# A one-core decoder layer on Trainium2: wide and narrow products of each split weight in strict alternation, high weights 192 bytes further in their tiles, and four smaller edits

## The chip, the core and the metric

One Trainium2 chip; the kernel runs on one of its cores. That core has TensorE (PE in the profile; its weight loads are the rows marked PEld), VectorE (DVE), ScalarE (ACT), GpSimd (POOL) and SyncE (SP), which issues most of the DMAs. Each engine works through its own queue in order and waits for the others by semaphores. The metric is the device time of one execution in microseconds, as a median over runs.

## The reference, cut to what matters

One layer over 256 positions of width 2048, everything in float32:

```python
h = rms_norm(x, pre_mix_norm)
gq, gk, gv, gz, ga, gb, mq, mk, mv = split(h @ w_in)          # 2048 x 7184
mix = concat([gdn(gq, gk, gv, gz, ga, gb), moba(mq, mk, mv)]) @ w_out   # 8 + 8 heads of 128
x = x + rms_norm(mix, post_mix_norm)
ca = cross_attention(rms_norm(x, pre_mem_norm), rms_norm(mem, mem_kv_norm))  # 4 heads, 256 tokens
x = x + rms_norm(ca, post_mem_norm)
f = square(relu(rms_norm(x, pre_mlp_norm) @ w_up)) @ w_down     # hidden 8192
x = x + rms_norm(f, post_mlp_norm)
```

Nearly all arithmetic is in the products with `w_in`, `w_out`, `w_up` and `w_down`.

## The kernel before

**Split products.** A float32 operand goes to TensorE as two fp32r parts, a high one (the rounded value) and a low one (the rest), and each product is high times high, high times low and low times high. Activations lie with their high and low part side by side, 256 + 256 columns. Weights arrive in float32 and are split on the way: `Stream` (line 51) cuts all weights into 434 units of 512 KB (the first four of 256 KB), loads each to `wraw` by SP, casts it to `whi` on ACT (L69) and subtracts it to `wlo` on DVE (L71). There are 5 `wraw`, 4 `whi` and 4 `wlo` buffers; a unit is asked for three units ahead (`AHEAD`).

**Two kinds of products.** Where the output is wanted transposed (`a_tile` and `a_group`, lines 118 to 140: the input projection but for `mv`, `w_mk`, `w_mq`, `w_up`), the weight is the stationary operand: `whi` streams 512 columns (both parts of the activation), `wlo` 256 columns (the high part alone). I call these two a wide and a narrow product, and together a pair: a pair is one 128x128 block of a weight. `products` (line 102) issues all wide ones of a unit first, then all narrow ones: eight and eight for a unit of 1024 columns. In `b_group` (`w_out`, `w_mv`, `w_mo`, `w_down`, `mv`) the activation is stationary and the weight streams, three products of 512 columns (256 in the halves of a last group) per block; the change leaves their order as it is.

**Order.** TensorE's queue stands as the code is written (`manual_schedule` of PE). DVE, ACT, SP and POOL are ordered by the framework's scheduler, but for what `pin` keeps in program order. Side work runs in generators on the list `bg`, which `tick` moves one step after each unit: the delta rule, the block attention `moba`, the memory's norm `mem_in`, and `natural`, which adds a residual in natural layout.

**Begin of the MLP.** After `w_mo`, `residual` (line 754) makes the row factors by Newton steps on DVE, scales the four 512-column slices of the result by them on ACT (L768, L772; DVE L769 for half of one), transposes two blocks at a time on TensorE (L778: one "pair of transposes" is four instructions), adds them to `x1` on DVE (L782) and splits the normed value (`norm_split`: ACT L231 high, DVE L232 low). The first `next(res)` makes the factors and scales slice 3; three more `next(res)` put four pairs of transposes in the queue with the idle products (`ones`) ahead of them; then `a_group` multiplies the first `w_up` unit (blocks 12 and 13), with one more pair of transposes behind each unit.

**Norm rows.** `row_load` (line 262) loads a norm weight to all partitions and scales it by the constant RS8 on ACT (L266).

## Time and profile before

| | us |
|---|---|
| median of 3 runs | 1317.57 (1316.19 to 1318.88) |
| the profiled execution | 1317.31 |
| its span, first to last instruction | 1315.5 |
| PE busy | 1295.0 of the span |
| DVE busy | 873.0 |
| ACT busy | 664.7 |
| time of the DMA queue with the weights | 56.3% of 16 engines |
| granted TensorE clock, mean | 0.995 |

The profiled execution took 0.26 us less than the median, and 1.8 us of it lie outside the span. A row of a list of groups gives line, engine, operation, names as out<-in, shapes and count, then busy time and the mean (or least, median, greatest) duration in ns. A row of a timeline gives start and length of a merged run in us, and in brackets the engine's idle time before it and what ended it. Ends of matmuls are modelled; spacings are therefore read from starts.

### The profile page before, as it was taken

What the parts mean: (1) busy time and instruction counts of PE and PEld (TensorE: products, weight loads), DVE (VectorE), ACT (ScalarE), POOL (GpSimd) and SP (SyncE); (2) the same over time, 40 slices, a digit from 0 to 9 for tenths busy, and PEclk for the clock granted to TensorE, in tenths of its full rate; (3) what the DMA queues carried; (4) which work ended last, traced back from release to release, by engine and by line L of the source; (5) the groups of instructions that cost most, each with busy time, mean ns of one, the idle gap of its engine ahead of it and who ended that gap; (6) DMA issues with size and microseconds to landing.
All of it is one profiled execution on the core that took longest, in us unless ns stands there. A gap on an engine that the chain in (4) does not pass through costs nothing.

```text
span 1315.5 us, 18643 instructions
## 1 busy us (share of the span) xinstructions
PE 1295.0 (98%) x6945; PEld 1115.1 (85%) x6945; DVE 873.0 (66%) x1528; ACT 664.7 (51%) x1028; POOL 35.4 (3%) x64
## 2 busy tenths in 40 slices
PE   9999999999999999999999999999999999999997
PEld 8888888898887788888888888888888888888886
DVE  8988879867575759759966654444466666554555
ACT  7655544525555757657644444444444444443442
POOL 1010010100000000000000000000000000000000
PEclk9999999999999999999999999999999999999998
DMA  8655565624446865744665656666655565666662
GB/s 308 190 183 182 187 192 172 194 82 144 144 130 224 290 213 169 246 154 145 196 190 191 191 178 195 196 192 195 196 193 189 184 190 191 214 198 193 193 190 86
DMA packets 72378, 246.25 MB, mean 187 GB/s; under 512 B 10408, under 2 KB 11872, under 8 KB 71904
## 3 DMA queue, kind: packets, MB, share of 16 engines
q1 hardware_dynamic: 70016, 239.27, 56.3%
q0 software_dynamic: 2272, 5.80, 1.5%
q8 instruction: 54, 0.88, 0.3%
q14 instruction: 36, 0.29, 0.1%
HBM read 241.35 MB, written 3.69 MB: 186 GB/s over the span
## 4 chain that ended last, share of the span: by engine, by line
PE 66%; DMA 3%; DVE 2%; ACT 1%; issue 1%; DVEq 0%; SPq 0%; ACTq 0%; POOLq 0%
PE mm L49 63%; PE ax L49 2%; DMA xs<-in_memT_dram 2%; DMA t<-rd 1%; DMA wraw<-in_wout_dram 1%; DVE wlo L71 1%; PE ax L778 0%; DVE ca L981 0%; ACT whi L69 0%; DMA rd<-t 0%; ACT m L231 0%; PE ax L886 0%; DVE fd L965 0%; DVE yg L681 0%; ACT ca L772 0%
## 5 line engine op out<-in xcount | busy, mean ns | idle before, releaser
L71 DVE TENSOR_TENSOR wlo<-wraw,whi 128x1024 fp32r<-128x1024 f32 (+1 forms) x434 | 528.1, 1219 | 371.7 <-ACT whi L69 369.6
L69 ACT ACTIVATE whi<-wraw 128x1024 fp32r<-128x1024 f32 (+1 forms) x434 | 456.2, 1054 | 519.2 <-PE mm L49 341.4
L49 PE MATMUL mm<-h,whi 128*128 128x512 f32 x1024 | 256.8, 393 | 0.0
L49 PE MATMUL mm<-whi,fp 128*128 128x512 f32 (+1 forms) x816 | 240.3, 377 | 0.0
L49 PEld LDWEIGHTS mm<-h,whi 128*128 128x128 f32 x1024 | 184.2, 189 | 33.2 <-DVE h L232 0.2
L49 PE MATMUL mm<-x,whi 128*128 128x512 f32 x768 | 201.0, 404 | 1.1 <-ACT whi L69 1.1
L49 PEld LDWEIGHTS mm<-whi,fp 128*128 128x128 f32 x816 | 150.2, 188 | 28.1
L49 PEld LDWEIGHTS mm<-x,whi 128*128 128x128 f32 x768 | 140.7, 191 | 27.6 <-ACT whi L69 1.5
L49 PE MATMUL mm<-wlo,fp 128*128 128x512 f32 (+1 forms) x408 | 153.7, 377 | 0.0
L49 PEld LDWEIGHTS mm<-h,wlo 128*128 128x128 f32 x1024 | 139.7, 190 | 10.0
L49 PE MATMUL mm<-h,wlo 128*128 128x256 f32 x1024 | 142.8, 282 | 0.0
L49 PEld LDWEIGHTS mm<-x,wlo 128*128 128x128 f32 x768 | 105.2, 190 | 8.0
L49 PE MATMUL mm<-x,wlo 128*128 128x256 f32 x768 | 107.4, 282 | 0.0
L49 PEld LDWEIGHTS mm<-wlo,fp 128*128 128x128 f32 x408 | 76.8, 188 | 14.2
L49 PE MATMUL mm<-whi,f 128*128 128x512 f32 (+1 forms) x272 | 81.0, 377 | 0.0
L49 PEld LDWEIGHTS mm<-whi,f 128*128 128x128 f32 x272 | 50.1, 188 | 9.4
L49 PE MATMUL mm<-wlo,f 128*128 128x512 f32 (+1 forms) x136 | 51.3, 377 | 0.0
L113 ACT ACTIVATE right<-mm 128x256 f32<-128x256 f32 x120 | 44.9, 378 | 4.6 <-PE mm L49 2.5
L49 PE MATMUL mm<-whi,ym 128*128 128x512 f32 x128 | 42.5, 393 | 0.9 <-ACT whi L69 0.9
L49 PE MATMUL mm<-whi,yg 128*128 128x512 f32 x128 | 41.9, 391 | 0.4 <-ACT whi L69 0.4
L381 DVE SCALAR_TENSOR_TENSOR t<-xc,cl,t 128x256 f32<-128x256 f32 x72 | 34.6, 481 | 2.6 <-ACT t L379 1.5
L49 PE MATMUL mm<-whi,x 128*128 128x512 f32 x96 | 31.8, 396 | 0.0
(359 smaller groups left out, 1246.8 us busy)
## 6 DMA issues: line engine op xcount, KB each, us to landing
wraw<-in_wup_dram SPq DMA_DIRECT2D x128, 512.0 KB, 3.9
wraw<-in_wdn_dram SPq DMA_DIRECT2D x128, 512.0 KB, 4.4
wraw<-in_win_dram SPq DMA_DIRECT2D x110, 512.0 KB, 4.0
wraw<-in_wout_dram SPq DMA_DIRECT2D x32, 512.0 KB, 5.0
wraw<-in_wmk_dram SPq DMA_DIRECT2D x8, 512.0 KB, 4.5
wraw<-in_wmq_dram SPq DMA_DIRECT2D x8, 512.0 KB, 4.2
wraw<-in_wmv_dram SPq DMA_DIRECT2D x8, 512.0 KB, 5.1
wraw<-in_wmo_dram SPq DMA_DIRECT2D x8, 512.0 KB, 3.7
```

Of the source, the lines that this page charges most:

```text
L49: TE.matmul(o, l, r, start=start, stop=stop, skip_group_check=skip)
L69: cast = S.activation(hi, r, AF.Copy)
L71: sub = V.tensor_tensor(lo, r, hi.bitcast(F32), OP.subtract)
L113: S.activation(t, o[:, T:], AF.Copy)
L381: V.scalar_tensor_tensor(y, c[:, i:i + T], cw[:, 4 * ch + i:4 * ch + i + 1], y, OP.mult, OP.add)
```

## The change

Five edits. (1) `three` takes the place of `products`: wide and narrow products alternate, one by one. (2) A `whi` tile has 1088 columns instead of 1024, and where the high weight is stationary it lies 48 columns (192 bytes) further in. (3) The MLP's first unit goes in three passes of 256 columns (high weight on the activation's high part, low weight on it, high weight on the low part), behind one pair of transposes and onto banks that a product with a tile of zeros has begun; ACT's scaling of a slice is put behind the first pair of transposes of the slice before; four units' casts and subtractions are pinned instead of one. (4) The norm rows stay unscaled and RS8 goes into the product that uses them. (5) `mem_in` splits its memory tokens in steps of two, `moba` waits one step more at its start, and a constant is put into `ssr` by a memset instead of an addition.

```diff
-            for n, (src, a, fine) in enumerate(plan):
+            for src, a, fine, off in plan:
                 step = 1 if fine else a // 2
-                s.units += [(n, src, a, k, step, fine) for k in range(0, a, step)]
+                s.units += [(src, a, k, step, off) for k in range(0, a, step)]
...
             nc.sync.dma_start(r, v[:, k:k + step])
-            hi = wp.tile([P, step, c], F32R, tag="whi", name="whi", bufs=NHI)
+            hi = wp.tile([P, 1024 + 64], F32R, tag="whi", name="whi", bufs=NHI)
+            hi = hi[:, off:off + step * c].rearrange("p (a c) -> p a c", a=step)
             cast = S.activation(hi, r, AF.Copy)
             lo = wp.tile([P, step, c], F32R, tag="wlo", name="wlo", bufs=NLO)
             sub = V.tensor_tensor(lo, r, hi.bitcast(F32), OP.subtract)
...
-    def products(steps):
-        for o, w, act, k, first, last in steps:
-            mm(o, w[0], act[2][k], start=first, stop=False)
-        for o, w, act, k, first, last in steps:
-            mm(o[:, :T], w[1], act[0][k], start=False, stop=last)
+    def three(o, whi, wlo, act, k, first, last):
+        mm(o, whi, act[2][k], start=first, stop=False)
+        mm(o[:, :T], wlo, act[0][k], start=False, stop=last)
...
         while k < KT:
-            u = ws.next()
-            products([(o, w, act, k + i, k + i == 0, k + i == KT - 1) for i, w in enumerate(u)])
-            k += len(u)
+            for w in ws.next():
+                three(o, *w, act, k, k == 0, k == KT - 1)
+                k += 1
             tick()
         return o
-    def a_group(act, order, pre=None):
...
-        o = [mmps() for _ in range(4)]
+    def a_group(act, order, pre=None, begun=None):
+        o = begun or [mmps() for _ in range(4)]
         n = 0
         while n < KT:
             u = ws.next()
             if pre:
                 pre(n)
-            cut = lambda w, c: [x[:, c * P:(c + 1) * P] for x in w]
-            products([(o[c], cut(w, c), act, order[n + i], n + i == 0, n + i == KT - 1)
-                      for i, w in enumerate(u) for c in range(4)])
-            n += len(u)
+            if begun and n == 0:
+                for kind in range(3):
+                    for i, w in enumerate(u):
+                        for c in range(4):
+                            cs = slice(c * P, (c + 1) * P)
+                            mm(o[c][:, T:] if kind == 2 else o[c][:, :T], w[kind % 2][:, cs],
+                               act[kind // 2][order[i]], start=False, stop=False)
+                    if kind == 1:
+                        pre(n)
+                n += len(u)
+                tick()
+                continue
+            for w in u:
+                for c in range(4):
+                    cs = slice(c * P, (c + 1) * P)
+                    three(o[c], w[0][:, cs], w[1][:, cs], act, order[n], n == 0, n == KT - 1)
+                n += 1
...
+    zero = cp.tile([P, P], F32R, name="zero")
     V.memset(ones, 1.0)
+    V.memset(zero.bitcast(F32), 0.0)
...
-    plan = [(win[i], 4, i == 0) for i in range(4)]
+    plan = [(win[i], 4, i == 0, 48) for i in range(4)]
     for what, h in TURNS:
         i, n = {"mv": (24 + 4 * h, 4), "kq": (2 * h, 2), "m": (32 + 2 * h, 2), "v": (16 + h, 1), "z": (48 + h, 1)}[what]
-        plan += [(win[i + j], 4 if what == "mv" else KT, False) for j in range(n)]
-    plan += [(wout[i], 4, False) for i in range(16)]
-    plan += [(wmk[i], KT, False) for i in range(HM)]
-    plan += [(wmq[i], 4, False) for i in range(HM)]
-    plan += [(wmv[i], 4, False) for i in range(4)]
-    plan += [(wmo[i], 4, False) for i in range(4)]
+        plan += [(win[i + j], *((4, False, 0) if what == "mv" else (KT, False, 48))) for j in range(n)]
+    plan += [(wout[i], 4, False, 0) for i in range(16)]
+    plan += [(wmk[i], KT, False, 48) for i in range(HM)]
+    plan += [(wmq[i], 4, False, 48) for i in range(HM)]
+    plan += [(wmv[i], 4, False, 0) for i in range(4)]
+    plan += [(wmo[i], 4, False, 0) for i in range(4)]
     for half in range(2):
-        plan += [(wup[32 * half + i], 4 if half == 0 and i < 4 else KT, False) for i in range(32)]
-        plan += [(wdn[32 * half + i], 4, False) for i in range(32)]
+        plan += [(wup[32 * half + i], 4 if half == 0 and i < 4 else KT, False, 48) for i in range(32)]
+        plan += [(wdn[32 * half + i], 4, False, 0) for i in range(32)]
...
         nc.sync.dma_start(w, bass.AP(tensor=rows.tensor, offset=rows.offset + i * D, ap=[[0, P], [1, D]]))
-        S.activation(w, w, AF.Copy, scale=RS8)
         return w
...
         ym = ap_.tile([P, 2, H, T], F32R, tag="ym", name="ym")
         def moba(h, q, k):
+            yield
             yield
...
-        ssr = small(10, "ssr")
+        ssr = small(12, "ssr")
         V.memset(ssr, 0.0)
+        V.memset(ssr[:, 5::6], D * EPS)
...
             V.tensor_reduce(ssq, ssr.rearrange("p (t c) -> p t c", t=2), AX.X, OP.add)
-            V.tensor_scalar(ssq, ssq, D * EPS, None, OP.add)
             r = newton8(ssq, name)
             for _ in range(lag):
                 yield
-            for n, c in enumerate((3, 0, 1, 2)):
...
-                        S.activation(m[t], m[t], AF.Copy, scale=r[:, t:t + 1])
+            m = {c: [src[:, t, 512 * c:512 * (c + 1)] for t in range(2)] for c in range(4)}
+            for i in range(2):
+                hc = slice(i * T, (i + 1) * T)
+                src0, src1 = [(o[i][0] if len(o) > 1 else o[0][0][:, hc]) for o in last]
+                S.activation(m[3][0][:, hc], src0, AF.Copy, scale=r[:, 0:1])
+                V.tensor_scalar(m[3][1][:, hc], src1, r[:, 1:2], None, OP.mult)
+            for c, then in ((3, 0), (0, 1), (1, 2), (2, None)):
                 for i in range(2):
                     yield
...
-        def natural(dst, other, i, r):
+                    if i == 0 and then is not None:
+                        for t in range(2):
+                            pin(S.activation(m[then][t], m[then][t], AF.Copy, scale=r[:, t:t + 1]))
...
-                    V.tensor_tensor(x, x, w[:, cs], OP.mult)
+                    late(V.scalar_tensor_tensor(x, x, RS8, w[:, cs], OP.mult, OP.mult))
                     V.tensor_tensor(x, x, o, OP.add)
...
                     sq = ld2.tile([P, 4, T], F32, tag="msq", name="msq", bufs=2) if q else acc
-                    prep(hm, memT, n_kv, ld2, 4 * q, 4, sq)
+                    xs = ld2.tile([P, 4, T], F32, tag="xs", name="xs", bufs=2)
+                    nc.sync.dma_start(xs, memT[q])
+                    for k in range(4):
+                        norm_split(hm, xs[:, k], n_kv, 4 * q + k)
+                        if k % 2:
+                            yield
+                    S.activation(sq, xs, AF.Square)
                     yield
                     if q:
                         V.tensor_tensor(acc, acc, sq, OP.add)
-                    yield
...
-                ssm.append(sm.tile([P, T], F32, tag="mmb", name="mmb"))
+                ssm.append(p2.tile([P, T], F32, tag="mmb", name="mmb"))
...
-        for _ in range(10):
+        for _ in range(9):
             mm(idle[:, 0:P], ones, ones)
-        for _ in range(3):
-            next(res)
+        begun = []
+        for n in range(4):
+            if n == 2:
+                next(res)
+            begun.append(mmps())
+            mm(begun[n], zero, chl[:, 0, 0:2].rearrange("p h t -> p (h t)"), stop=False)
...
-        ws.pin, ws.ahead = 1, AHEAD
-        o_first = a_group(h2, late, lambda n: next(res, None))
+        ws.pin, ws.ahead = 4, AHEAD
+        o_first = a_group(h2, late, lambda n: next(res, None), begun)
...
-        bg.append(natural(x2n, lambda t, cs: mix[:, t, cs], 1, r2))
+        bg.append(natural(x2n, lambda t, cs: mix[:, t, cs], 1, r2, pin))
...
-                    V.tensor_tensor(fw[t, c], fd[:, t, cs], wrow[:, cs], OP.mult)
+                    V.scalar_tensor_tensor(fw[t, c], fd[:, t, cs], RS8, wrow[:, cs], OP.mult, OP.mult)
```

TensorE in the up projection, at any unit (`h` is the normed activation). Before:

```order
L49 MATMUL mm<-h_6036,whi 128x512 x8
L49 MATMUL mm<-h_6036,wlo 128x256 x8
L49 MATMUL mm<-h_6036,whi 128x512 x8
L49 MATMUL mm<-h_6036,wlo 128x256 x8
L49 MATMUL mm<-h_6036,whi 128x512 x8
```

The same place now:

```order
L49 MATMUL mm<-h_6037,whi 128x512
L49 MATMUL mm<-h_6037,wlo 128x256
L49 MATMUL mm<-h_6037,whi 128x512
L49 MATMUL mm<-h_6037,wlo 128x256
L49 MATMUL mm<-h_6037,whi 128x512
L49 MATMUL mm<-h_6037,wlo 128x256
```

Nothing but the order within a unit moved: the count of wide and of narrow products is the same.

TensorE at the begin of the MLP (`ca` is the attention's result, transposed against `ident`). Before:

```order
L49 MATMUL ax<-ones 128x128 x10
L778 MATMUL ax<-ident,ca 128x128 x16
L49 MATMUL mm<-h_6036,whi 128x512 x8
L49 MATMUL mm<-h_6036,wlo 128x256 x8
L778 MATMUL ax<-ident,ca 128x128 x4
L49 MATMUL mm<-h_6036,whi 128x512 x8
```

And now:

```order
L49 MATMUL ax<-ones 128x128 x9
L49 MATMUL mm<-chl,zero 128x512 x2
L788 MATMUL ax<-ident,ca 128x128 x4
L49 MATMUL mm<-chl,zero 128x512 x2
L788 MATMUL ax<-ident,ca 128x128 x4
L49 MATMUL mm<-h_6037,whi 128x256 x8
L49 MATMUL mm<-h_6037,wlo 128x256 x8
L788 MATMUL ax<-ident,ca 128x128 x4
L49 MATMUL mm<-h_6037,whi 128x256 x8
L788 MATMUL ax<-ident,ca 128x128 x4
L49 MATMUL mm<-h_6037,whi 128x512
```

Two pairs of transposes stand ahead of the first weight product instead of four, and two more within the first unit.

ACT there, from the scaling of slice 3 on. Before:

```order
L768 ACTIVATE ca<-mm,x_6040 128x256 x2
L772 ACTIVATE ca<-ca,x_6040 128x512 x2
L231 ACTIVATE h_6036<-x_4445,cl 128x256 x3
L772 ACTIVATE ca<-ca,x_6040 128x512 x2
L231 ACTIVATE h_6036<-x_4445,cl 128x256 x3
L69 ACTIVATE whi<-wraw 128x1024 x2
```

And now:

```order
L780 ACTIVATE ca<-mm,x_6040 128x256 x2
L244 ACTIVATE h_6037<-x_4447,cl 128x256 x2
L797 ACTIVATE ca<-ca,x_6040 128x512 x2
L70 ACTIVATE whi<-wraw 128x1024 x2
L244 ACTIVATE h_6037<-x_4447,cl 128x256 x4
L797 ACTIVATE ca<-ca,x_6040 128x512 x2
```

The splits of blocks 12 and 13 moved ahead of the scaling of slice 0, and two casts ahead of the splits of blocks 14 and 15. DVE's queue there, before:

```order
L782 SCALAR_TENSOR_TENSOR x_4445<-ax,n_sc,x_4445 128x256 x3
L232 SCALAR_TENSOR_TENSOR h_6036<-x_4445,cl,h_6036 128x256 x2
L782 SCALAR_TENSOR_TENSOR x_4445<-ax,n_sc,x_4445 128x256
L232 SCALAR_TENSOR_TENSOR h_6036<-x_4445,cl,h_6036 128x256
L782 SCALAR_TENSOR_TENSOR x_4445<-ax,n_sc,x_4445 128x256 x2
```

And now:

```order
L792 SCALAR_TENSOR_TENSOR x_4447<-ax,n_sc,x_4447 128x256 x3
L245 SCALAR_TENSOR_TENSOR h_6037<-x_4447,cl,h_6037 128x256 x2
L792 SCALAR_TENSOR_TENSOR x_4447<-ax,n_sc,x_4447 128x256 x2
L72 TENSOR_TENSOR wlo<-wraw,whi 128x1024 x2
L245 SCALAR_TENSOR_TENSOR h_6037<-x_4447,cl,h_6037 128x256 x3
```

The two subtractions that belong to those casts now stand ahead of the low part of block 14. At the memory's norm, the queues of ACT and DVE stand as before but for their line numbers.

## Rows read from the trace of the kernel before

**Rows 1.** The page: busy us of each engine, share of the span, instructions.

```profile
PE 1295.0 (98%) x6945; PEld 1115.1 (85%) x6945; DVE 873.0 (66%) x1528; ACT 664.7 (51%) x1028; POOL 35.4 (3%) x64
```

**Rows 2.** Timeline of PE in the up projection: start us, us, what.

```profile
640.44 2.00 PE L49 MATMUL mm<-h,whi 128*128 128x512 f32 x8
642.28 1.11 PE L49 MATMUL mm<-h,wlo 128*128 128x256 f32 x8
...
648.82 2.00 PE L49 MATMUL mm<-h,whi 128*128 128x512 f32 x8
```

**Rows 3.** By tile: count, durations in ns (least/median/greatest), first and last start.

```profile
L49 PE MATMUL mm<-h,whi x1024: 387/393/496, 596.7 to 1129.0; 128*128 128x512 f32 x171
L49 PE MATMUL mm<-x,whi x768: 387/393/774, 5.0 to 393.6; 128*128 128x512 f32 x192
L49 PE MATMUL mm<-whi,f x272: 277/389/396, 777.3 to 1271.9; 128*128 128x512 f32 x120, 128*128 128x256 f32 x16
```

**Rows 4.** By tile, the same view for the low parts.

```profile
L49 PE MATMUL mm<-h,wlo x1024: 277/283/283, 598.6 to 1130.0; 128*128 128x256 f32 x171
```

**Rows 5.** Timeline of PE in the `mv` products, 512 columns throughout.

```profile
38.16 0.39 PE L49 MATMUL mm<-wlo,x 128*128 128x512 f32 x1
...
40.20 0.39 PE L49 MATMUL ax<-wlo,x 128*128 128x512 f32 x1
```

**Rows 6.** Timeline of PE in the last `w_down` group: six of 512 columns, twelve of 256.

```profile
1272.00 0.40 PE L49 MATMUL mm<-whi,fp 128*128 128x512 f32 x1
...
1273.16 0.50 PE L49 MATMUL mm<-whi,fp 128*128 128x512 f32 x2
...
1273.98 0.40 PE L49 MATMUL mm<-whi,fp 128*128 128x256 f32 x2
...
1274.70 0.52 PE L49 MATMUL mm<-whi,fp 128*128 128x256 f32 x2
```

**Rows 7.** Timeline of PE at the start of the program.

```profile
12.27 2.11 PE L49 MATMUL mm<-x,whi 128*128 128x512 f32 x8 [0.72 <-ACT whi L69]
...
15.17 2.01 PE L49 MATMUL mm<-x,whi 128*128 128x512 f32 x8
```

**Rows 8.** Timeline of DVE in the same stretch.

```profile
12.25 1.23 DVE L71 TENSOR_TENSOR wlo<-wraw,whi 128x1024 fp32r<-128x1024 f32 x1 [1.02 <-ACT whi L69]
...
15.59 1.22 DVE L71 TENSOR_TENSOR wlo<-wraw,whi 128x1024 fp32r<-128x1024 f32 x1
```

**Rows 9.** Timeline of all engines at the begin of the MLP.

```profile
594.37 1.33 ACT L772 ACTIVATE ca<-ca,x 128x512 f32<-128x512 f32 x2
...
594.89 1.27 DVE L782 SCALAR_TENSOR_TENSOR x<-ax,n_sc,x 128x256 f32<-128x256 f32 x3 [0.25 <-PE ax L778]
595.60 1.30 ACT L231 ACTIVATE h<-x,cl 128x256 fp32r<-128x256 f32 x3
...
596.67 2.11 PE L49 MATMUL mm<-h,whi 128*128 128x512 f32 x8
...
599.22 2.00 ACT L69 ACTIVATE whi<-wraw 128x1024 fp32r<-128x1024 f32 x2
...
599.93 1.40 PE L49 MATMUL mm<-h,whi 128*128 128x512 f32 x5
```

**Rows 10.** Chain of waits in order of time, at 446 us.

```profile
445.78 9.56 DMA wraw<-in_wout_dram
```

**Rows 11.** Timeline of ACT there, and of PE behind it.

```profile
454.10 1.92 ACT L266 ACTIVATE wrow<-wrow 128x2048 f32<-128x2048 f32 x1 [7.10 <-DMA wrow<-in_rows_dram]
...
457.01 0.49 PE L49 MATMUL mm<-whi,yg 128*128 128x512 f32 x1 [0.44 <-ACT whi L69]
```

**Rows 12.** Timeline of PE at a fall of the clock.

```profile
273.10 1.10 PE L49 MATMUL ax<-tr,ga 128*128 128x64 f32 x8 [0.84 <-DVE t L550]
274.01 3.63 PE L49 MATMUL mm<-x,whi 128*128 128x512 f32 x8
```

**Rows 13.** A window there: length, busy us (count) of PE, PEld, DVE, ACT, POOL, then the granted clock.

```profile
274.10:277.40 3.30, 3.30 (x9) 2.57 (x9) 0.86 (x4) 0.00 (x0) 0.00 (x0) 0.51 0.01 5
```

More of the change, by code (lines that the diff above doesn't have):

```diff
@@ L57, in __init__ @@
             s.units, s.done, s.pos, s.pin, s.ahead = [], [], 0, 0, AHEAD
-            for n, (src, a, fine) in enumerate(plan):
+            for src, a, fine, off in plan:
                 step = 1 if fine else a // 2
-                s.units += [(n, src, a, k, step, fine) for k in range(0, a, step)]
+                s.units += [(src, a, k, step, off) for k in range(0, a, step)]
         def emit(s):
-            n, src, a, k, step, fine = s.units[len(s.done)]
+            src, a, k, step, off = s.units[len(s.done)]
             v = src.rearrange("p (a c) -> p a c", a=a)
@@ L749, in stat_out @@
                     jk = p2.tile([P, 512], F32, tag="jk", name="jk")
-                    S.activation(jk[:, cs], b, AF.Square, accum_out=ssr[:, 5 * t + c + i:5 * t + c + i + 1])
+                    S.activation(jk[:, cs], b, AF.Square, accum_out=ssr[:, 6 * t + c + i:6 * t + c + i + 1])
                     if c < 3:
@@ L761, in residual @@
                 yield
-            for n, c in enumerate((3, 0, 1, 2)):
-                m = [src[:, t, 512 * c:512 * (c + 1)] for t in range(2)]
-                if c == 3:
-                    for i in range(2):
-                        hc = slice(i * T, (i + 1) * T)
-                        src0, src1 = [(o[i][0] if len(o) > 1 else o[0][0][:, hc]) for o in last]
-                        S.activation(m[0][:, hc], src0, AF.Copy, scale=r[:, 0:1])
-                        V.tensor_scalar(m[1][:, hc], src1, r[:, 1:2], None, OP.mult)
-                else:
-                    for t in range(2):
-                        S.activation(m[t], m[t], AF.Copy, scale=r[:, t:t + 1])
+            m = {c: [src[:, t, 512 * c:512 * (c + 1)] for t in range(2)] for c in range(4)}
[5 more added lines that the diff above has]
+            for c, then in ((3, 0), (0, 1), (1, 2), (2, None)):
                 for i in range(2):
@@ L778, in residual @@
                             TE.transpose(pT[:, j * T + t * P:j * T + (t + 1) * P],
-                                         m[t][:, (2 * i + j) * P:(2 * i + j + 1) * P], ident)
+                                         m[c][t][:, (2 * i + j) * P:(2 * i + j + 1) * P], ident)
                     for j in range(2):
@@ L784, in residual, with natural @@
                         norm_split(act, x1[:, k], ncol, k)
-        def natural(dst, other, i, r):
+                    if i == 0 and then is not None:
+                        for t in range(2):
+                            pin(S.activation(m[then][t], m[then][t], AF.Copy, scale=r[:, t:t + 1]))
+        def natural(dst, other, i, r, late=lambda x: x):
             ssx = small(8, "ssx")
@@ L826, in mem_in @@
                         V.tensor_tensor(acc, acc, sq, OP.add)
-                    yield
-                    yield
                 fold(acc)
```

## The prediction

> **What bounds the kernel now.** I read the page's busy times first: PE is busy for 1295.0 of the span's 1315.5 us [rows 1]. No transfer or vector engine can be the limit over long stretches; what counts is the pace of TensorE's own products, and a few stalls. So the second view is the spacing of products, from starts. In the up projection a unit of eight wide and eight narrow ones recurs every (648.82 - 640.44) / 3 = 2.793 us, 349.2 ns a pair [rows 2]. Third, is that the least? Where products of 512 columns follow each other they start every 2.04 / 9 = 227 ns [rows 5]. Narrow ones inside a long run start every 0.72 / 6 = 120 ns [rows 6]. Eight wide ones at 227 and eight narrow at 120 would make 2.773 us; the unit takes 20 ns more. The reason shows where runs of both widths take turns in another product: right behind twelve narrow ones the first five wide ones are spaced 1.16 / 5 = 232 ns, 5 ns over the settled pace [rows 6]. Durations agree: wide ones of the up projection have a median of 393 ns, those of the down projection 389 [rows 3]. So a run of narrow products leaves something that slows the next wide ones, whatever the operands are. The narrow ones are not at their least either: the shortest lasts 277 ns, the median 283 [rows 4], and the eight of a unit take 2.793 less the 1.84 us of the wide ones, 0.95 us, where eight at 120 ns are 0.96 [rows 2]. Both say that one of them, which must be the first behind the wide run, is 6 to 10 ns shorter than the others: I put it at 114 ns.
>
> **Alternation, and the shifted high weights.** There are 1024 pairs in the up projection and 768 in the input projection [rows 3], and 128 more of the same form in `w_mk` and `w_mq` (eight units each of eight pairs, by the code), 1920 in all; eight of them go another way at the begin of the MLP, so 1912 alternate. Each narrow product is now the first behind a wide one, and no wide one stands behind a run. If the wide one keeps its 227 ns and the narrow one the 114 of a first, a pair costs 341 ns (340.7 unrounded), 8.5 less than 349.2: 1912 x 8.5 = 16.3 us. The trace has no wide product behind exactly one narrow one, so I bound it. From above: if one narrow product disturbs as a run does, the wide one takes the 232 and the narrow one behind a disturbed one 118 to 120: 350 to 352 ns, a loss of 1.5 to 5.4 us. From below: the least durations lie 2 ns under the settled wide one and 6 under the median narrow one [rows 3, 4], which gives 225 + 112 = 337, a gain of 23 us. In between, if the narrow one always takes 120 because a weight load lies under it: 347 ns, a gain of 4.2. I take 341, since it is what both rows say of a product that is not part of a narrow run, and the disturbance took a run of eight or twelve in every row I have. For the 192 bytes no row has a price: the down projection, whose operands lie elsewhere, settles at the same duration of 389 as the `mv` products [rows 3, 5], so I give the shift nothing, and both bounds above hold for it.
>
> A row and a rule differ here. Products of 512 columns, undisturbed, are spaced 227 ns [rows 5], 14 more than their columns take at 2.4 GHz. The Trainium skill (TensorE: Matmul & The Clock Gate, Back-to-back issue gap) gives N / 2.4 + 2.5 ns, an estimate of 216 for 512 columns and 109 for 256, so 325 ns a pair and 46 us less. The trace does not agree with it for these fp32r products.
>
> **What alternation adds.** The second product of a unit now needs `wlo`, which before was wanted only behind eight wide ones, 1.84 us later [rows 2]. In steady stretches units are made three ahead and it lies ready. At the start it does not. The unit at 12.27 had its low part at 12.25 + 1.23 = 13.48 [rows 7, 8]; alternating, it wants it at 12.50 and waits 1.0 us. The next, from 15.17 on, then begins at 16.2; its low part is there at 16.81 [rows 8], 0.4 to 0.5 after it is wanted. What the four small units before lose is swallowed by the 0.72 us wait for the cast ahead of 12.27 [rows 7]. The third unit of 512 KB then starts about 1.5 us later. Behind TensorE wait only evictions, so the cost is **+1.5** (0.5 to 2).
>
> **Begin of the MLP.** Now the first products stood at 596.67, behind four pairs of transposes; the second unit started at 599.93 [rows 9]. With one pair ahead, DVE adds block 12 from 594.89 in 0.40 us steps, and ACT, which no longer scales slice 0 first, splits blocks 12 and 13 from about 595.3 (0.43 each): the passes can begin at 595.8, 0.9 us sooner. But what ACT did then comes later. Slice 0 (1.33) runs to 597.5, and the two pinned casts (2.00) to 599.5, ahead of the high part of block 14. On DVE the subtractions of these casts stand ahead of the low part of block 14: the second can start at 599.5 at the earliest and ends by 600.8 to 601.1 (1.22 each [rows 8]), then 0.43 for block 14: the second unit starts at 601.2 to 601.5 where it was 599.93. The products of the first unit, 24 of 256 columns at 120 ns, are 2.88 us against 2.79, hidden in that wait, and so are the products with zeros. Net **+1.4**, bounds -0.9 (the queue catches up) and +1.6.
>
> **Norm rows.** In the output projection ACT waited 7.10 us for the row and scaled it for 1.92, until 456.0, and TensorE then waited for the cast behind it [rows 11]. Without the scaling, the cast waits for its own transfer, which landed at 445.78 + 9.56 = 455.34 [rows 10]: 0.5 us sooner, **-0.5**. The two other rows lie in stretches where no product waits for them; the product with RS8 takes the place of one multiplication on DVE.
>
> **Memory in steps, `moba`, `ssr`.** The queues of ACT and DVE at the memory stand as before, so its stalls stay: nothing. `moba` one step later moves small products by a unit among the stalls at 270 to 370 us. One of them had TensorE's clock fall from 2.4 to 1.2 GHz: after 24 products of 64 columns, 0.84 us of idleness and eight more, eight wide ones took 3.63 us at a clock of 0.51 instead of 2.00 [rows 2, 12, 13]. Such a fall costs 1.6 us; I expect as many as before, and one more or less in the range.
>
> **Sum.** 1317.3 for the profiled execution, which is 0.3 under the median of the runs, - 16.3 + 1.5 + 1.4 - 0.5 = 1303.4; I forecast **1303 us**.
>
> **Rivals.** (a) *The weight load keeps the narrow one at 120 ns.* For it: 120 ns is the pace of every narrow run [rows 6]. Against: the first of a run is shorter [rows 4]. The pair is 347 ns: 1317.3 - 4.2 + 2.4 = 1315.5. (b) *One narrow product disturbs as much as eight*, the slower side: every wide product then stays at 232 and every narrow one behind it at 118 to 120, so that the pair costs 350 to 352. For it: the first wide one behind a run is among the slowest. Against: the disturbance fades over several products, so it has been built up. It gives 1321 to 1325, and decides above 348 ns a pair, where alternation no longer pays for the 2.4 us of the other edits. (c) *The shift does what the rows can't show*, and both widths fall to their least, 337 ns: 1317.3 - 23 + 2.4 = 1297, or a little under. (d) *Products cost their columns alone*: 213 + 107 = 320 ns at 2.4 GHz, 1317.3 - 55.8 + 2.4 = 1264. No row comes near it. (The rule of the Trainium skill named above would have it at 1273.)
>
> **How the numbers follow.** The forecast 0.47, (a) 0.19, (b) 0.22, (c) 0.10, (d) 0.02. The bounds of the start, of the MLP's begin and of a clock's fall add 3 us to either side of each. The range from 1296 to 1321 leaves out (d), part of (c) and the upper half of (b), some 0.19. A measurement of this kernel can tell about 0.2% from no change, 2.6 us. Faster by more: the forecast, (c), (d) and half of (a), 0.68. Within: the other half of (a) and the lower end of (b), 0.17. Slower: the rest of (b), 0.15.
>
> **What would show it.** Right: alternating pairs in the up projection start every 341 ns, with 227 behind a wide one and 114 behind a narrow one. For (a) the narrow step reads 120, for (b) the wide step 232 or more, for (c) the sum is under 338. The start is right if the third unit of 512 KB begins 1.5 us later, the MLP if its second unit waits for DVE's low part at 601. The forecast is wrong if products that alternate have a spacing of their own that no run of equal ones shows, or if the shift of 192 bytes sets it.

## The result, and the profile after

The changed kernel takes 1300.35 us (median of 4 runs, 1299.73 to 1301.94), the kernel before 1317.92 beside it: a ratio of 0.9875 (95% interval 0.986 to 0.989), 17.6 us less. The forecast was 1303, in a range from 1296 to 1321. The profiled execution took 1301.94, with a span of 1300.2 us, 15.4 less than the one before.

The page's first row, busy us of each engine, answers [rows 1]: PE is busy for 15.6 us less, and the other engines have not moved by more than 5; the weight loads (PEld), which lie under the products, by 11.

```profile
PE 1279.4 (98%) x6955; PEld 1103.9 (85%) x6955; DVE 873.7 (67%) x1528; ACT 659.7 (51%) x1025; POOL 35.6 (3%) x64
```

Timeline of PE in the up projection (start us, length, what), in answer to [rows 2]; the last row is the 24th wide product behind the first:

```profile
639.77 0.39 PE L49 MATMUL mm<-h,whi 128*128 128x512 f32 x1
640.00 0.28 PE L49 MATMUL mm<-h,wlo 128*128 128x256 f32 x1
640.11 0.39 PE L49 MATMUL mm<-h,whi 128*128 128x512 f32 x1
...
647.93 0.39 PE L49 MATMUL mm<-h,whi 128*128 128x512 f32 x1
```

24 pairs take 8.16 us: 340 ns each, where they took 349.2 [rows 2]. The wide step is 0.23, the narrow one 0.11, as forecast. But not everywhere. The same view in the input projection:

```profile
213.28 0.40 PE L49 MATMUL mm<-x,whi 128*128 128x512 f32 x1
213.52 0.28 PE L49 MATMUL mm<-x,wlo 128*128 128x256 f32 x1
213.63 0.40 PE L49 MATMUL mm<-x,whi 128*128 128x512 f32 x1
...
214.69 0.40 PE L49 MATMUL mm<-x,whi 128*128 128x512 f32 x1
```

Four pairs there take 1.41 us, 350 ns each or a little over. Four units in a row (from 207.8 us on) keep this pace, after which the quick one returns. Alternation has more than one pace, and something decides between them that the prediction did not have.

The program's start, PE and then DVE, in answer to [rows 7, 8]: the second product of a unit waits for the low weights, 0.77 us at 14.18 and 0.26 at 17.51, and DVE makes them from 12.90 and 16.23 on.

```profile
12.92 0.49 PE L49 MATMUL mm<-x,whi 128*128 128x512 f32 x1 [0.53 <-ACT whi L70]
14.18 0.39 PE L49 MATMUL mm<-x,wlo 128*128 128x256 f32 x1 [0.77 <-DVE wlo L72]
...
17.51 0.38 PE L49 MATMUL mm<-x,wlo 128*128 128x256 f32 x1 [0.26 <-DVE wlo L72]
```

```profile
12.90 1.22 DVE L72 TENSOR_TENSOR wlo<-wraw,whi 128x1024 fp32r<-128x1024 f32 x1 [1.30 <-ACT whi L70]
...
16.23 1.22 DVE L72 TENSOR_TENSOR wlo<-wraw,whi 128x1024 fp32r<-128x1024 f32 x1
```

The begin of the MLP, all engines, in answer to [rows 9], and behind it the window of the products that follow (length, busy us and count of PE, granted clock, DMA share, GB/s):

```profile
587.31 1.99 ACT L70 ACTIVATE whi<-wraw 128x1024 fp32r<-128x1024 f32 x2
...
588.87 2.35 DVE L72 TENSOR_TENSOR wlo<-wraw,whi 128x1024 fp32r<-128x1024 f32 x2
...
589.20 1.29 ACT L244 ACTIVATE h<-x,cl 128x256 fp32r<-128x256 f32 x3
...
591.14 1.27 DVE L245 SCALAR_TENSOR_TENSOR h<-x,cl,h 128x256 fp32r<-128x256 f32 x3
...
591.67 0.70 PE L49 MATMUL mm<-h,whi 128*128 128x512 f32 x1 [1.85 <-DVE h L245]
```

```profile
591.60:595.00 3.40, 3.33 (x11) 0.53 0.74 254
```

ACT's two casts stand ahead of its split of block 14 and DVE's two subtractions ahead of the low part, and TensorE waits 1.85 us for that. Then the clock is at 0.53 of its full rate (the 1.2 GHz level) for ten products. In the trace of before there is no fall here; its two falls, at 274 and 373 us, are gone.

### The profile page after: what moved, and what is told of

Its sections match the earlier page's. It is cut to its first block, busy times and chain, and to the rows that moved or that the text cites. A ratio compares the mean times of both kernels' runs of the same rounds, so it can differ in the third digit from the quotient of the medians.

```text
span 1300.2 us, 18654 instructions
## 1 busy us (share of the span) xinstructions
PE 1279.4 (98%) x6955; PEld 1103.9 (85%) x6955; DVE 873.7 (67%) x1528; ACT 659.7 (51%) x1025; POOL 35.6 (3%) x64
## 4 chain that ended last, share of the span: by engine, by line
PE 65%; DVE 2%; DMA 2%; issue 1%; ACT 0%; DVEq 0%; SPq 0%; POOL 0%; ACTq 0%; POOLq 0%
PE mm L49 63%; DMA xs<-in_memT_dram 1%; PE ax L49 1%; DVE wlo L72 1%; PE ax L788 0%; DMA t<-rd 0%; DVE ca L1003 0%; PE ax L903 0%; ACT whi L70 0%; DVE fd L987 0%; DVE yg L695 0%; ACT fj L989 0%; DVE m L245 0%; DVE t L693 0%; DVE fr L206 0%
## 5 line engine op out<-in xcount | busy, mean ns | idle before, releaser
L49 PE MATMUL mm<-h,whi 128*128 128x512 f32 (+1 forms) x1032 | 350.2, 389 | 2.1 <-DVE h L245 1.9
L49 PE MATMUL mm<-h,wlo 128*128 128x256 f32 x1024 | 282.3, 277 | 0.0
L49 PE MATMUL mm<-x,whi 128*128 128x512 f32 x768 | 270.6, 397 | 0.8 <-ACT whi L70 0.8
L49 PEld LDWEIGHTS mm<-h,whi 128*128 128x128 f32 x1032 | 193.5, 188 | 42.1 <-DVE h L245 2.1
L49 PE MATMUL mm<-x,wlo 128*128 128x256 f32 x768 | 213.2, 278 | 1.5 <-DVE wlo L72 1.5
L49 PEld LDWEIGHTS mm<-h,wlo 128*128 128x128 f32 x1024 | 192.6, 189 | 0.0
L49 PEld LDWEIGHTS mm<-x,whi 128*128 128x128 f32 x768 | 144.3, 188 | 30.4 <-ACT whi L70 1.3
L49 PEld LDWEIGHTS mm<-x,wlo 128*128 128x128 f32 x768 | 144.3, 188 | 3.3 <-DVE wlo L72 2.7
```

Of the source, the lines that this page charges most:

```text
L49: TE.matmul(o, l, r, start=start, stop=stop, skip_group_check=skip)
```

## The experiments

All times below are medians beside runs of the kernel before on the same chip; a ratio is to that. Two kernels of different groups ran on different chips, so small differences between them are also followed in the traces, from product to product.

**Alternation and shift, apart.** First alternation alone, in the kernel before:

```diff
         for o, w, act, k, first, last in steps:
             mm(o, w[0], act[2][k], start=first, stop=False)
-        for o, w, act, k, first, last in steps:
             mm(o[:, :T], w[1], act[0][k], start=False, stop=last)
```

> The kernel before, with nothing but strict alternation (high weights where they were). In the trace of the changed kernel a pair of the up projection takes 227 + 113 = 340 ns throughout, but in the input projection some units, as the four from 207.8 us on, run at 233 + 117 = 350 ns from end to end: alternation has two paces. Theory A (alternation alone does it, as the prediction has it: the shift has no price): most pairs at 340 to 341 ns, 1317.6 - 16.3 + 2.1 at the start = 1303 us. Theory B (the shift is what keeps the pairs at the quick pace): most pairs stay at 350 ns, which is no gain over 349.2, and with the start it takes 1319 to 1322 us.

Measured: 1321.76 us, ratio 1.0041 (1.0026 to 1.0056): *slower* than before. PE in the up projection, three pairs in a row and a row 24 pairs behind the first:

```profile
649.57 0.40 PE L49 MATMUL mm<-h,whi 128*128 128x512 f32 x1
649.81 0.28 PE L49 MATMUL mm<-h,wlo 128*128 128x256 f32 x1
649.93 0.40 PE L49 MATMUL mm<-h,whi 128*128 128x512 f32 x1
650.17 0.28 PE L49 MATMUL mm<-h,wlo 128*128 128x256 f32 x1
650.28 0.40 PE L49 MATMUL mm<-h,whi 128*128 128x512 f32 x1
...
658.05 0.40 PE L49 MATMUL mm<-h,whi 128*128 128x512 f32 x1
```

8.48 us for 24 pairs: 353 ns. The wide step is 0.24 and the narrow one up to 0.12: with the operands at these places, each narrow product disturbs the wide one behind it. Theory A falls. Then with the shift:

```diff
-            hi = wp.tile([P, step, c], F32R, tag="whi", name="whi", bufs=NHI)
+            hi = wp.tile([P, 1024 + 64], F32R, tag="whi", name="whi", bufs=NHI)
+            hi = hi[:, off:off + step * c].rearrange("p (a c) -> p a c", a=step)
...
+    ws = Stream([(*p, 48 if st else 0) for p, st in zip(plan, stat)])
```

(`stat` is true where the weight is stationary.)

> The kernel before with alternation and the high weights 48 columns (192 bytes) further in tiles of 1088 columns, none of the other edits. Theory A and theory B both: pairs at 340 ns but for some ten units of the input projection, 1317.6 - 16 + 2.1 = 1303 to 1304 us. If the other edits of the change together gain (their sum was forecast at +0.9 without the start), it is slower than the changed kernel by that; if they lose, it is quicker than the changed kernel's 1300.4 us, down to 1298.

Measured: 1302.73 us, ratio 0.9896 (0.9881 to 0.9911), 24 pairs in 8.16 us:

```profile
639.97 0.39 PE L49 MATMUL mm<-h,whi 128*128 128x512 f32 x1
...
648.13 0.39 PE L49 MATMUL mm<-h,whi 128*128 128x512 f32 x1
```

The loads of the weights last 188 ns by the median in both runs, within 1 ns; what gets longer without the shift are the products themselves (medians 398 and 281 ns by their modelled ends, against 389 and 276). Then the shift alone, with runs of eight kept:

> The kernel before with the high weights 192 bytes further, and still eight wide products and then eight narrow ones. Theory A (the shift has no price): 2.793 us a unit of sixteen products, 1317.6 us, within 2.6. Theory C (the place of the high weights sets the pace of every product, whatever the order): the wide ones behind a narrow run are at 227 at once, a unit takes 2.77 us or less, 1312 to 1313 us, and lower if the narrow ones fall under 120 ns too.

Measured: 1316.66 us, ratio 0.9999 (0.9989 to 1.001). A unit takes (648.73 - 640.37) / 3 = 2.787 us, 348.3 ns a pair, against 349.2 (in the second half of the MLP 349.1, as before):

```profile
640.37 2.01 PE L49 MATMUL mm<-h,whi 128*128 128x512 f32 x8
...
648.73 2.01 PE L49 MATMUL mm<-h,whi 128*128 128x512 f32 x8
```

So alternation alone loses 4.9 us, the shift alone gives nothing, and the two together give 14: the gain is of the pair of edits, not of either.

**The begin of the MLP undone** in the changed kernel:

```diff
-        for _ in range(9):
+        for _ in range(10):
             mm(idle[:, 0:P], ones, ones)
...
+        for _ in range(3):
+            next(res)
...
-        ws.pin, ws.ahead = 4, AHEAD
-        o_first = a_group(h2, late, lambda n: next(res, None), begun)
+        ws.pin, ws.ahead = 1, AHEAD
+        o_first = a_group(h2, late, lambda n: next(res, None))
```

> The changed kernel with the MLP begun as before: four pairs of transposes ahead of the first product, slices scaled ahead of them, one unit's cast pinned, no products with zeros. In the changed kernel's trace TensorE waits 1.85 us for the split of block 14 behind the first unit, then runs ten products at half clock (about 1.4 us). Prediction (the new begin costs 1.4 us, more with the fall of the clock): 1297 to 1299 us, and no fall of the clock there. Rival (the wait and the fall only move what the begin costs anyway, and the old one leaves 0.9 us more idle ahead of the first product): 1300 to 1301.5 us.

Measured: 1297.14 us (1296.87 to 1298.64), ratio 0.9854 (0.984 to 0.9869), 3.2 us under the changed kernel. In its trace no product waits there for `h`, and the clock does not fall. From the same late product of `w_mo` to the fourth `w_up` unit the changed kernel takes 22.2 us and this one 18.7. So the new begin costs 3.2 us net by the medians, 3.5 in the two traces.

**Which places are quick.** In the kernel before, high weights, low weights and activations all begin 64 bytes past a multiple of 256 by my count of the tiles that lie ahead of them; no trace shows an address, and the places named below rest on this count. That the three lie alike modulo 256 follows from the sizes of the tiles. Three more shifts of the high weights (`off` 16, 32, 64 columns), and one of the low weights by 48, each with alternation (the first one's edit; in the last, `wlo` has the wider tile instead of `whi`):

```diff
-    ws = Stream([(*p, 48 if st else 0) for p, st in zip(plan, stat)])
+    ws = Stream([(*p, 16 if st else 0) for p, st in zip(plan, stat)])
```

> The kernel before with alternation, high weights 16 columns (64 bytes) further instead of 48. Without a shift a pair of the up projection took 353 ns (1321.8 us), with 192 bytes 340 (1302.7 us). All other operands of these products begin 64 bytes past a multiple of 256; a shift of 192 brings the high weights onto the multiple, one of 64 to 128 past it. Theory P (the place itself counts: the multiple of 256 is quick): slow, 350 to 353 ns, 1319 to 1322 us. Theory D (the high weight must only lie otherwise than the low weight and the moving operand, modulo 256): quick, 340 ns, 1302 to 1304 us.

> The same with 32 columns (128 bytes): the high weights lie 192 past a multiple of 256, the other operands 64. Theory P: 350 to 353 ns a pair, 1319 to 1322 us. Theory D: 340 ns, 1302 to 1304 us. A value in between in this run or the one with 64 bytes would say that the distance is graded.

> The same with 64 columns (256 bytes): the high weights lie 64 past a multiple of 256 as all others do, but in tiles of 1088 columns as in the quick kernel. Theories P and D: no gain from it, 350 to 353 ns a pair, 1319 to 1322 us. Rival (it was the larger tile, which puts every second buffer 256 bytes further, or any distance from where they lay): 340 ns, 1303 us, at least in every second unit.

> The kernel before with alternation, and the low weights instead of the high ones 48 columns (192 bytes) further. Theory D: 340 ns a pair, 1302 to 1304 us, since high and low weights differ by as much as before. Theory P, if it is the wide products' weights that must lie on the multiple: 353 ns, 1321 us. Theory P, if either width profits by itself: between, about 346 ns, 1311 us.

Measured, one run each, the kernel before at 1317.32: 1314.15, 1321.77, 1322.45 and 1319.94 us. The times hold falls of the clock too (the last run's mean granted clock is 0.992, the third's 0.998), so the spacing is what to read. 24 pairs take 8.45 us with 32 columns (352 ns) and 8.48 with 64 (353): a shift by 256 bytes is none, and the larger tile does nothing. The low weights shifted give 8.32 us (347 ns) in the first half of the MLP and 8.40 (350) in the second, so moving the low ones gains a little at best:

```profile
649.85 0.40 PE L49 MATMUL mm<-h,whi 128*128 128x512 f32 x1
...
658.17 0.40 PE L49 MATMUL mm<-h,whi 128*128 128x512 f32 x1
```

Neither theory holds as it was put: P has no quick pace but on the multiple, D has all of these quick but the third. The first and the last of the four have the same distance of 64 bytes between high and low weights; they differ in which of the two the activations lie with. The run with 16 columns is the telling one. PE in its two halves of the MLP, 24 pairs each:

```profile
699.67 0.39 PE L49 MATMUL mm<-h,whi 128*128 128x512 f32 x1
...
708.07 0.39 PE L49 MATMUL mm<-h,whi 128*128 128x512 f32 x1
```

```profile
999.51 0.39 PE L49 MATMUL mm<-h,whi 128*128 128x512 f32 x1
...
1007.67 0.39 PE L49 MATMUL mm<-h,whi 128*128 128x512 f32 x1
```

8.40 us (350 ns) in the first half, from the sixth unit on without exception (transposes stand among the first five), and 8.16 (340 ns) in the second. It is the same loop over the same places, and the other engines are no busier: DVE 63% from 700 to 776 us and 65% from 960 to 1030, ACT 48 and 49%. So one order of products has several paces, and each keeps itself up; the input projection of this run even has a third, with most units at 354 ns. How the stream is entered seems to decide. After the program's first units, undisturbed units run at the quick pace only from 60, 191 and 953 us on, each time behind a long run of products of 512 columns, and the run with the low weights shifted changes its pace at the same three places (to 350, from 347). But no run here changed the entry alone, so this is a reading, not shown. The slow units of the changed kernel's input projection come behind small products; most units that do are quick.

Then the place itself against the places' distances. Based on the kernel with the old begin, tiles of 1024 columns again, and unused tiles ahead of the weights and of the activations:

```diff
+    wp.tile([P, 48], F32, name="wpad", tag="wpad")
+    ap_.tile([P, 16], F32, name="apad", tag="apad")
     ws = Stream(plan)
```

(the first run has the first line alone).

> The changed kernel with the old begin of the MLP (1297.1 us), high-weight tiles of 1024 columns again, and instead of the shift one unused tile of 48 columns ahead of all weight tiles: high weights, low weights and activations then all lie on multiples of 256 bytes; so far only the high weights did, the others 64 bytes past. Theory P (each product is quickest with its operands on a multiple of 256): 340 ns a pair, and the ten or so units of the input projection that ran at 350 do so no more: 1296 us. Theory R (what counts is that the weight and the moving operand begin at different places modulo 256): as without a shift, 353 ns, about 1315 us.

> The same with a second unused tile of 16 columns ahead of the activations: high and low weights on multiples of 256 bytes, activations 64 past one. Theory P: 340 ns a pair, 1296 to 1297 us. Theory R, between weight and moving operand: 340 ns, 1296 to 1297 us. Theory R, if it is high against low weights that must differ: 350 to 353 ns, 1313 to 1316 us. With the run before, in which all three agree, it tells these apart.

Measured: 1318.58 us, ratio 1.001 (0.9998 to 1.0023), and 1331.36, ratio 1.0101 (1.007 to 1.0131), where the kernel they are made from takes 1297.14. Both need 8.48 us for 24 pairs, 353 ns: PE of the second,

```profile
649.71 0.40 PE L49 MATMUL mm<-h,whi 128*128 128x512 f32 x1
...
658.19 0.40 PE L49 MATMUL mm<-h,whi 128*128 128x512 f32 x1
```

Theory P falls: on the multiple, all three are as slow as 64 past it. So does theory R between weight and moving operand: in the second run these differ, and it is slow. The reading that is left is that high and low weights must not lie alike modulo 256, and that not every distance will do: 192 and (in the second half of the MLP) 64 bytes were quick, 128 was not, and the low ones moved instead hardly were. Why, these runs don't tell.

The second run lost 13 us more than the first, and the down projection shows where the most of it went (its two halves take 5.1 and 3.7 us longer). Its wide products by tile (count, least/median/greatest ns), with the activation stationary and the weight moving, in the kernel with the old begin and in this one:

```profile
L49 PE MATMUL mm<-whi,fp x816: 277/389/396, 772.9 to 1285.7; 128*128 128x512 f32 x144, 128*128 128x256 f32 x20
```

```profile
L49 PE MATMUL mm<-whi,fp x816: 280/393/398, 792.0 to 1320.1; 128*128 128x512 f32 x144, 128*128 128x256 f32 x20
```

389 ns against 393; from starts, the mean step of neighbours of 512 columns is 226.9 against 233.3. There all neighbours are equally wide, and moving and stationary operand, alike in all other kernels but for multiples of 256, had been set 64 bytes apart. So the settled pace of 227 ns is itself a matter of places.

**The small edits.** The kernel with alternation and shift alone takes 1302.73 us, the one with all but the new begin 1297.14; the step that `moba` waits longer was taken out of the latter:

```diff
         def moba(h, q, k):
             yield
-            yield
             pS = aux()
```

> The changed kernel with the old begin of the MLP, and the block attention one step earlier, as before the change. The prediction gave this step nothing. Alternation and the shift alone took 1302.7 us, and with the small edits (norm rows, memory in steps, the later block attention) 1297.1; in the trace without them TensorE stands still 0.88, 0.56 and 0.87 us at 216.5, 230.1 and 285.4 us behind small products that wait, and 0.0 there with them. If the later step is what takes these waits away: 1299 to 1299.5 us. If the prediction is right and it is another of these edits: 1297 us.

Measured: 1302.74 us (1301.97 to 1304.30), ratio 0.9886 (0.9853 to 0.9919): in this kernel one `yield` is worth 5.6 us by the medians. Between the same products, from 206 to 301 us, the two traces part by 5.9 us. TensorE's waits from 200 to 300 us (engine line, waited for: us in total, times, longest us), where the kernel with the `yield` has none at all, and the longest of them:

```profile
PE ax L49 <- DVE t L274: 2.2, 3, 1.6
PE ax L49 <- DVE ym L673: 0.7, 1, 0.7
```

```profile
218.85 0.92 PE L49 MATMUL ax<-t,t 128*128 128x128 f32 x4 [1.59 <-DVE t L274]
```

Those four are `moba`'s first products; they wait for the scaled tile `t` that DVE writes in its own time behind a subtraction:

```profile
216.92 1.21 DVE L72 TENSOR_TENSOR wlo<-wraw,whi 128x1024 fp32r<-128x1024 f32 x1
218.06 0.41 DVE L523 TENSOR_TENSOR t<-ntb 64x256 f32<-64x256 f32 x1
218.39 0.41 DVE L274 SCALAR_TENSOR_TENSOR t<-right,x0b 128x256 f32<-128x256 f32 x1
```

One step later, `t` is there. Behind the wait that ends at 287.7, for `ym`, which `moba` writes, the clock then falls for eight pairs (seven of the wide steps 0.2 us longer). So about half of the 5.9 us is waits (2.9) and the rest this fall.

That the 5.6 us are all that the small edits gain is not shown, though the medians of this kernel and of alternation and shift alone agree. The latter has the early step too, but no fall there: against the kernel with the `yield` it loses only 1.9 us from 206 to 301 us, and 2.3 more from 405 to 488, at the memory and in the output projection, where this one loses 0.7. There its clock is low for 6.8 us, against 3.4 in the two others, so the traces leave open what the norm rows and the memory's steps are worth.

In the kernel before no product of PE waits from 200 to 268 us, even with the early step. Alternation brings these waits, even at its slow pace (0.3 us for `t` in the run of alternation alone), and the quicker products make them longer. The wait for `ym` was there before, at another place; TensorE's waits from 200 to 390 us in the kernel before have it:

```profile
PE ax L49 <- DVE ym L660: 1.6, 1, 1.6
```

It ends at 372.7 us, ahead of the second fall of the clock. No kernel with the later step waits for `ym`.

**The start undone**, in the kernel with the old begin:

```diff
+            if ws.pos in (5, 6):
+                for kind in range(2):
+                    for i, w in enumerate(u):
+                        for c in range(4):
+                            mm(o[c][:, :T] if kind else o[c], w[kind][:, c * P:(c + 1) * P], act[2 - 2 * kind][order[n + i]],
...
             for w in u:
```

> The changed kernel with the old begin of the MLP (1297.1 us, the quickest so far), and at the program's start the two first units of 512 KB multiplied as before: eight wide products, then eight narrow ones. Prediction's step (the low part is wanted earlier than DVE makes it, 1.5 us in its working; in the trace with the old begin TensorE waits 0.77 and 0.33 us for it there, and stands 1.5 us behind the kernel before at the third of these units): these waits go, sixteen pairs cost some 9 ns more each, and the third unit begins about 1.3 us earlier: 1295.8 us. Rival (the time is only moved, since the units behind wait for the casts and subtractions in any case): 1297.1 us, and a wait at the third or fourth unit instead.

Measured: 1297.21 us, ratio 0.9849 (0.9828 to 0.987). PE shows the third unit at 17.97, 1.5 us sooner than 19.50, and a wait of 0.44 there instead:

```profile
12.28 2.12 PE L49 MATMUL mm<-x,whi 128*128 128x512 f32 x8
...
17.97 0.39 PE L49 MATMUL mm<-x,whi 128*128 128x512 f32 x1
18.80 0.38 PE L49 MATMUL mm<-x,wlo 128*128 128x256 f32 x1 [0.44 <-DVE wlo L72]
```

The next unit is 0.8 ahead, and so is every product up to 405 us. Then the lead is gone. TensorE's waits at the memory, 408 to 432 us, of this run and, in the second fence, of the one it was made from:

```profile
PE mm L49 <- DVE wlo L72: 2.7, 4, 0.8
PE mm L49 <- ACT whi L70: 0.4, 1, 0.4
```

```profile
PE mm L49 <- ACT whi L70: 1.2, 1, 1.2
PE mm L49 <- DVE wlo L72: 0.8, 1, 0.8
```

3.1 us of waits against 2.0, and in the second the clock fell as well, for eight steps that are 1.6 us longer in all; behind both, the same product stands at 443.6 and 443.4. The chain of waits of the changed kernel runs there through the memory's transfers:

```profile
404.02 10.57 DMA xs<-in_memT_dram
415.03 1.05 ACT whi L70
```

That whoever is early waits longer for these transfers is my reading of it. By the medians the rival holds (1297.21 and 1297.14 us, where 1.3 us were forecast), but the interval, 2.8 us to either side, does not exclude the forecast. Nor do the traces agree on it: the lead over the changed kernel, which has the new start and no fall of the clock at the memory, shrinks from 1.5 us at 405 to 1.1 at 488 and 0.8 at 569 us, so a part is left. The version that beats both kernels is the changed kernel with the old begin of the MLP, at 1297.1; the start in runs adds nothing to it that can be told.

## Why the prediction was right, point by point

- **The number is right, and the largest term has the right size for a reason that the prediction denied.** It put alternation at 341 ns and gave the shift nothing. Measured: 353 ns and +4.9 us without the shift, 340 with it. That the two edits together give what alternation alone was to give is luck: by the prediction's own last sign, "if the shift of 192 bytes sets it", its mechanism is wrong. What alternation does by itself is rival (b), nearly to the number (350 to 352 ns, 1321 to 1325 us): where the operands lie alike, a single narrow product disturbs the next wide one as a run does. The step that failed is the sentence on the 192 bytes, that the down projection, "whose operands lie elsewhere", settles at the same duration. Modulo 256 they lie alike, by the same count of tiles: weights and activations at 64, in every product of the kernel before. No row of before could price the shift, and it belonged in the sum with both ends, not at zero.
- **The steps themselves** were read well: 227 and 114 ns are what both products take undisturbed, by the rows of before, and 227 and 113 is what they take with the high weights 192 bytes further. The lower bound, 337 a pair, was not reached.
- **The size, -16.3.** The up projection gave 9.2 ns a pair in its steady stretch. Of the 96 units of the input projection twelve stay at 350 ns, and many have their first pairs disturbed behind small products. By the mean steps from starts, with wide steps over 300 ns and narrow ones over 160 left out as stalls, a pair of the up projection went from 349.1 to 340.2 ns (1016 pairs, 9.0 us), one of the input projection from 349.1 to 342.1 (768, 5.4 us), and the 128 others gave 0.9: 15.3 us.
- **Start, +1.5.** In the trace the third unit begins 2.1 us later (20.11 against 17.97), since the smaller units before it wait as well, and that was said to be swallowed; in the other traces with this start it is 1.5 to 1.9. How much of it is left at the end is open: the run that undid it gained nothing by its median, and its trace keeps a part.
- **Begin of the MLP, +1.4.** The mechanism is right in each step: casts and subtractions ahead of block 14, and a wait for DVE's low part. Counted from the same late product of `w_mo` (577.41 us, before 587.35), the second unit starts 14.3 us on, before 12.6 [rows 9]: 1.7 later, against 1.3 to 1.6 forecast. The size is off by what stands behind: the clock fell after the wait, and ten products, most of them at half rate, took 3.3 us instead of 1.7, another 1.6. The medians put the edit at 3.2. The prediction had falls in its range only as "one more or less", and did not connect one with the wait that it forecast itself.
- **Norm rows, -0.5.** TensorE's waits at 456 us [rows 11] are gone: none is left from 440 to 452 in the changed kernel. But alternation and shift alone, with the rows scaled, wait only 0.3 us there, so by that trace the edit is worth no more.
- **`moba`, 0.** Wrong: without the longer step the kernel with the old begin takes 5.6 us more. The term was priced without the waits that alternation brings at `moba`'s first products, and without the 1.6 us wait for its output `ym` that the trace of before has.
- **Falls of the clock: as many as before.** In the profiled executions two at 270 to 380 us went, one came at the MLP. At 1.6 us each by the prediction's price, the two are 3.2 us; with TensorE's waits there, 3.7 us before and 2.2 after, some 4.7 us went that the sum had at nothing. What part of it the longer step of `moba` did, no run tells.

So the sum held partly by luck. In the two traces, 15.4 us apart, the pairs gave about 1 us less than forecast and the begin of the MLP cost 1.8 more, and the 4.7 us of waits and falls that went in the input projection made up for both. One rule of the Trainium skill (TensorE: Matmul & The Clock Gate, Step-by-step: what each phase is for) would have spoken for giving the shift nothing: loading the next weights takes no SBUF read bandwidth from the running product, since each has a port of its own. With nothing but the tiles' beginnings changed, the runs here take 340 and 353 ns a pair, and it is the products that get longer, not the loads; by what way the places act, no run shows.

## What to carry to other kernels

Where products of two widths take turns, try order and place of their operands together: neither had a gain by itself here, and the wrong place cost 1% (1331 us) even with the right order. Before a resource is called free because "every row agrees", ask whether the rows differ in it at all. And price a small edit in the kernel that it will stand in: a wait that isn't there yet, such as the one at `moba`'s first products, comes when the work around it changes, while time won ahead of a later wait, as at the start, may not last to the end.

## What was not expected of the hardware

- Alternating products of 512 and 256 columns have two steady paces, 340 and 350 ns a pair, in the same loop over the same tiles; each lasted some 60 units on end (up projection, shift of 64 bytes).
- The beginnings of operands modulo 256 bytes change the spacing of products by 4% (340 against 353 ns), with the same instructions on TensorE, while the weight loads last 188 ns at either pace; moving all of them alike (64 bytes past the multiple, or on it) changes nothing.
- Equally wide products feel it too: in the down projection 393 instead of 389 ns, and a mean step of 233 instead of 227, when stationary and moving operand lie 64 bytes apart. What in the chip makes it so is open.
